# Attention's value products of two units issued as one row, into two halves of one PSUM bank

## The chip, the cores and the metric

The kernel runs on one core of one Trainium2 chip. The metric is the device time of one execution in microseconds (us); the time of a kernel is the median of its runs. The profile is one execution taken by the hardware profiler. Its engines are TensorE (PE; its weight loads are listed apart, as PEld), VectorE (DVE), ScalarE (ACT), GpSimd (POOL) and the queues that issue DMAs, above all SyncE's (SP).

## The reference

Two layers of a block that mixes a 1024-token grid (16 rows of 64) and 256 context tokens in three ways: neighbourhood attention with 8 heads, a bidirectional mLSTM and a Hyena long convolution. What the change touches is the attention:

```python
def row_block(r):
    ...
    s = jnp.concatenate([s_lat..., s_ctx], axis=-1)
    p = jax.nn.softmax(s, axis=-1).astype(v.dtype)
    ...
    o = jnp.einsum('bhjqic,bijchd->bjqhd', p_lat, vw) + jnp.einsum('bhjqn,bnhd->bjqhd', p_ctx, vc)
```

Around it stand `mod = silu(c) @ w_ada + b_ada` (shift, scale and gate of a layer), the input projection `h @ w_in`, and `y @ w_out` with a norm and a gate. In layer 0 the context tokens go through an attention of their own as well. All is in float32.

## The kernel before

All PE work stands in one fixed order, made when the program is built. Each part of the block is a Python generator; `flow` keeps a list of them sorted by rank and lets the first one go on whose time has come by `Clock`, a model of the engines that is advanced as instructions are written down. A generator hands back the tiles it needs, a name that another one will `announce`, or a time; `want` waits until a PSUM bank of a tag is free by that model (`BANKS`: two of `pj`, three of `s`, two of `tp`, one of `o`). So a change in one generator moves the rows of all others. DVE, ACT, POOL and the DMA queues run in the order that comes out too.

- `projections` (rank 2, the last) fills every gap with the input projection: `pj` tiles, each 8 steps of 3 fp32r products, 128x512 or 128x256 wide. 2496 such products belong to layer 0, 1968 to layer 1. The last blocks of a layer (24, 22, 25 and 23: gates of the mLSTM output) end in tiles `sz` and `so` that are written to the DRAM tensor `yp`.
- `na` is the attention. `keys` and `values` load a head; four copies of `work` (rank 1) take units in turn: 8 heads x 5 units in layer 0 (four blocks of 16 grid columns and the context), 8 x 4 in layer 1. A unit makes scores (`apl`, `apc`), a softmax on DVE, ACT and POOL (`ae`), 10 transposes (`apt`, in three groups; a context unit has one group of 4) that are copied to `ph`, and the value products `apo`. These use 64 of the 128 columns of the array, so two of them, one for PSUM partitions 0 to 63 and one for 64 to 127, run side by side; a group is such a pair, 256 or (third group) 128 wide. An fp32 product is two instructions in the trace, so a pair is four. ACT copies one half of the result to `at`, DVE adds it to the other half into `ay`. When a pair of heads is done ("closing"), `az` is `ay` times a gate, and goes to `yp`.
- In `before` the three groups of a unit alternate with the transposes of the next group and with waits for the neighbouring unit (`pv...`), and each group is issued when its `ph` part is there.
- `ada_late` (rank 1.2, after `work`) runs in layer 0's attention: 16 groups `ada`, each 8 products of 32 columns on two tiles `wada` of 512 KB. There are two such tiles in all, so the loads of a group wait for the products of the group before. Each group takes a `tp` bank. Its end (`adas`) is awaited before the attention counts as done (`N0`).
- `out_early` loads `w_out` (8 tiles `wos`, four at a time), splits it (`woh` on ACT; `wol` on DVE for every second one if `N` of the layer is known by then, else all on POOL), as soon as `P` (projections written down) or `N` is known. Then `out_proj` runs the products `op` on `yh`, `yl`, made from `gr`, which is loaded from `yp`.

```python
            raw = []
...
            (nc.vector if i % 2 and f"N{l}" in self.known else nc.gpsimd).tensor_tensor(out=wl[:, b, :], in0=raw[i], in1=wh[:, b, :].bitcast(F32), op=ALU.subtract)
```

The two lines that set the pace of `ada_late`:

```python
                    tiles.append(pool.tile([128, 1024], F32, name=f"wada_{l2}_{part2}_{kt2}", tag="wad", bufs=2))
...
                yield tiles[j], tiles[j + 1], 1.0
                yield from self.want("tp")
```

Of the kernel before, what the change touches and what calls it, by code (L numbers as in the profile page):

```python
# [13 lines left out]
F32 = mybir.dt.float32  # L14
# [3 lines left out]
ALU = mybir.AluOpType  # L18
# [5 lines left out]
L, LC = 1024, 256  # L24
LT = L + LC
# [8 lines left out]
QA, KA, VA, ZA = 0, 4, 8, 12  # L34
# [126 lines left out]
class Kern:  # L161
# [1085 lines left out]
    def na(self, l, pool, upd):  # L1247

        nc = self.nc
        HP = [slice(0, 64), slice(64, 128)]  # L1250
        heads, vals, ys, bias, left = {}, {}, {}, {}, {}
# [61 lines left out]
        def work():  # L1313
            while units:
                turn = 8 * nu - len(units)
                hd, cb = units.pop(0)
                pr, h = hd // 2, hd % 2
                p, o = HP[h], HP[1 - h]
                nme = f"{l}_{hd}_{cb}"
                types = [hf * 3 + (0 if cb == 0 else (2 if cb == 3 else 1)) for hf in range(2)] if cb < 4 else []  # L1320
                for ty in types:
                    if (hd, ty) not in bias:
                        bias[hd, ty] = pool.tile([128, 384], F32, name=f"ab{l}_{hd}_{ty}", tag="ab", bufs=3)
                        nc.sync.dma_start(out=bias[hd, ty], in_=self.I["nab"][l, hd, ty])
# [2 lines left out]
                    ys[hd] = ys[hd + 1] = pool.tile([128, LT], F32, name=f"ay{l}_{pr}", tag="ay", bufs=1)  # L1327
                y = ys[hd]
                qs, kh, kl = heads[hd]
                yield from self.want("s", qs, kh, kl, extra=2.0)  # L1330
                pc = self.bank("s", f"apc{nme}")
                E = []
                st = pool.tile([128, 8, 2], F32, name=f"ast{nme}", tag="ast", bufs=3)
                lat = cb < 4
                q0 = cb * 256 if lat else L
                pls = []
                for hf in range(2):
                    q = qs[:, q0 + hf * 128:q0 + hf * 128 + 128]
                    if lat:
                        cs = slice(CB_START[cb], CB_START[cb] + 32)  # L1340
# [31 lines left out]
                a, b, f = slice(0, 256), slice(256, 512), slice(0, 256)  # L1372
                groups = [([blk(0, 3), blk(1, 3), blk(0, 4), blk(1, 4)], [(0, a, f), (1, b, f)])]
# [3 lines left out]
                ng = len(groups)  # L1377
                closing = h == 1 and cb == nu - 1
                ne = LT if upd else L
                parts = []  # L1380

                for gi in range(ng + 1):
                    if turn and gi < ng:
                        yield f"pv{l}_{turn - 1}_{min(gi + 1, 2)}"
                    if gi < ng:
                        yield from self.want("tp")
                        tp = self.bank("tp", f"apt{nme}_{gi}")
                        for j, x in enumerate(groups[gi][0]):
                            self.tr(out=tp[:, j * 128:(j + 1) * 128], in_=x, identity=self.ident)
                        x = pool.tile([128, 512], F32, name=f"ph{nme}_{gi}", tag="ph", bufs=3)  # L1390
                        w = len(groups[gi][0]) * 128
                        (nc.vector.tensor_copy if gi == 1 else nc.scalar.copy)(x[:, :w], tp[:, :w])
                        parts.append(x)
                    if gi == ng - 1 and closing:
                        yield f"b{l}_{ZA + pr}"
                        zs = []
                        for x in range(0, ne, ne // 2):
                            z = pool.tile([128, 640], F32, name=f"az{l}_{pr}_{x}", tag="ae", bufs=8)[:, 0:ne // 2]
                            nc.sync.dma_start(out=z, in_=self.GT[l][pr][:, x:x + ne // 2])
                            zs.append((slice(x, x + ne // 2), z))  # L1400
                    if gi == 0:
                        continue
                    if gi == 1:
                        if turn:
                            yield f"pv{l}_{turn - 1}_3"
                        yield f"hv{l}_{hd}_{cb if lat else -1}"
                        vc, vb = vals[hd, -1], vals.get((hd, cb))
                        yield from self.want("o", vc)
# [7 lines left out]
                for gi in range(ng, 4):  # L1416
                    self.announce(f"pv{l}_{turn}_{gi}")
                self.announce(f"nv{l}_{hd}_{cb}")
                t = pool.tile([128, 256], F32, name=f"at{nme}", tag="at", bufs=2)
                nc.scalar.copy(t[p], po[o, 0:256])  # L1420
                if lat:
                    yv = grid(y)[p, :, 16 * cb:16 * cb + 16]
                    shp = lambda t: t.rearrange("p (r c) -> p r c", c=16)
                else:
                    yv, shp = y[p, L:LT], lambda t: t
                nc.vector.tensor_tensor(out=yv, in0=shp(po[p, 0:256]), in1=shp(t[p]), op=ALU.add)
# [13 lines left out]
        for w in range(4):  # L1440
            self.spawn(work(), 1)
# [541 lines left out]

# [9 lines left out]
```

## Time and profile before

| what | value |
|---|---|
| median of 3 runs | 1974.19 us (1967.37 to 1975.5) |
| the profiled execution | 1969.88 us, of it 1968.1 us from first to last instruction |
| PE busy | 1857.6 us, 94% of the span |
| DVE, ACT, POOL busy | 1058.3, 786.8, 461.3 us (54%, 40%, 23%) |
| mean granted PE clock | 0.976 |

The profiled execution is 4.3 us below the median. The attention of layer 0 runs from about 680 to 992 us, that of layer 1 from about 1560 to 1840 us. A busy PE is not yet a PE at its peak: what a product really holds up is read from the distance between the starts of two instructions.

### The profile page before, as it was taken

To read this page: it belongs to the slowest core of one execution; us is meant where nothing else is said; L and a number is where in the kernel's file an instruction comes from. 1 tells how busy PE (TensorE), PEld (TensorE's weight loads), DVE (VectorE), ACT (ScalarE), POOL (GpSimd) and SP (SyncE) were. 2 spreads that over 40 slices of the span, in tenths; PEclk is the share of its full clock that TensorE was granted. 3 is DMA by queue.
4 is the path that set the end of the run, shared out by engine and by line. 5 is a ranking of instruction groups with operands and counts; after the bars stand their busy time and mean duration, and the time that the engine had idled before them with its cause. 6 is when DMAs were issued, how large, how long until landed. Compare 5 with 4: busy or idle time off the path is not lost. (4 is left out here: it accounts for less than half of the span.)

```text
span 1968.1 us, 28340 instructions
## 1 busy us (share of the span) xinstructions
PE 1857.6 (94%) x10008; PEld 1418.7 (72%) x10008; DVE 1058.3 (54%) x2398; ACT 786.8 (40%) x1545; POOL 461.3 (23%) x368
## 2 busy tenths in 40 slices
PE   8699989998999899999999999899899999999998
PEld 2465867787788776777777886678677867676776
DVE  3744454537736366677545544444762476666533
ACT  3645342414423254444434444332323255454321
POOL 1534111314220121121222122222412122122300
PEclk9799999999999999999999999999899999999999
DMA  8476888863221557666354357765222455454543
GB/s 315 141 241 211 287 228 242 231 231 107 80 82 45 178 149 216 201 212 217 105 192 139 139 159 217 221 194 172 77 80 82 133 160 161 125 161 131 181 130 107
DMA packets 233610, 328.91 MB, mean 167 GB/s; under 512 B 22509, under 2 KB 162185, under 8 KB 231550
## 3 DMA queue, kind: packets, MB, share of 16 engines
q1 hardware_dynamic: 186942, 264.45, 44.0%
q10 hardware_dynamic: 46528, 62.67, 9.1%
q8 instruction: 79, 1.29, 0.3%
q14 instruction: 61, 0.50, 0.1%
HBM read 230.82 MB, written 96.21 MB: 166 GB/s over the span
## 5 line engine op out<-in xcount | busy, mean ns | idle before, releaser
L182 PE MATMUL pj<-hhi,wh 128*128 128x512 f32 (+2 forms) x1504 | 598.5, 398 | 4.9 <-ACT sv L155 4.9
L182 PE MATMUL pj<-hlo,wh 128*128 128x512 f32 (+2 forms) x1504 | 550.3, 366 | 0.1
L182 PE MATMUL pj<-hhi,wl 128*128 128x512 f32 (+1 forms) x1456 | 535.1, 368 | 0.0
L182 PEld LDWEIGHTS pj<-hhi,wh 128*128 128x128 f32 (+1 forms) x1504 | 285.7, 190 | 71.3 <-issue 29.5
L182 PEld LDWEIGHTS pj<-hlo,wh 128*128 128x128 f32 (+1 forms) x1504 | 285.4, 190 | 46.2 <-issue 9.4
L182 PEld LDWEIGHTS pj<-hhi,wl 128*128 128x128 f32 x1456 | 277.5, 191 | 46.6
L155 POOL TENSOR_TENSOR wl<-wr,wh 128x1024 fp32r<-128x1024 f32 x68 | 165.2, 2429 | 541.1 <-ACT wh L155 511.8
L155 POOL TENSOR_SCALAR ae<-ae,ast 128x640 f32<-128x640 f32 (+1 forms) x72 | 69.4, 964 | 411.0 <-DVE ast L155 313.5
L155 ACT ACTIVATE ae<-ae,ast 128x640 f32<-128x640 f32 (+1 forms) x144 | 113.1, 787 | 106.6 <-DVE ast L155 100.7
L182 PE MATMUL op<-woh,yh 128*128 128x512 f32 x288 | 115.4, 401 | 9.7 <-ACT yh L155 9.7
L182 PE MATMUL apo<-ph,aVn 128*64 128x256 f32 (+1 forms) x800 | 113.7, 369 | 4.0 <-DVE ph L155 1.5
L182 PE MATMUL op<-woh,yl 128*128 128x512 f32 x288 | 114.7, 398 | 0.9 <-DVE yl L155 0.8
L182 PE MATMUL op<-wol,yh 128*128 128x512 f32 x288 | 114.4, 397 | 0.0
L155 ACT CAST wh<-wr 128x1024 fp32r<-128x1024 f32 (+1 forms) x70 | 72.0, 1028 | 103.9 <-PE pj L182 88.6
L155 ACT COPY ph<-apt 128x512 f32<-128x512 f32 (+1 forms) x136 | 65.6, 483 | 112.3 <-PE apt L186 111.8
L186 PE MATMUL apt<-ident,ae 128*128 128x128 f32 x672 | 109.0, 281 | 0.4 <-DVE ph L155 0.3
L186 PEld LDWEIGHTS apt<-ident,ae 128*128 128x128 f32 x672 | 76.9, 141 | 35.8 <-issue 25.1
L155 ACT COPY sr<-pj 128x512 f32<-128x512 f32 (+3 forms) x94 | 49.3, 525 | 133.2 <-PE pj L182 125.3
L155 DVE CUSTOM_DVE_ANT_0 ae<-apl,ab 128x384 f32<-128x384 f32 x128 | 69.5, 552 | 53.8 <-PE apl L182 32.5
L182 PEld LDWEIGHTS apo<-ph,aVn 128*64 128x64 f32 x800 | 40.8, 135 | 53.9 <-issue 29.2
L182 PEld LDWEIGHTS op<-woh,yh 128*128 128x128 f32 x288 | 55.5, 193 | 21.8 <-ACT yh L155 10.6
L182 PEld LDWEIGHTS op<-woh,yl 128*128 128x128 f32 x288 | 55.4, 192 | 14.2 <-DVE yl L155 2.7
(255 smaller groups left out, 3030.4 us busy)
## 6 DMA issues: line engine op xcount, KB each, us to landing
wr<-in_wblk SPq DMA_DIRECT2D x68, 512.0 KB
wada<-in_wada SPq DMA_DIRECT2D x48, 512.0 KB
ab<-in_nab SPq DMA_DIRECT2D x96, 192.0 KB
pr<-sr ACTq DMA_DIRECT2D x64, 256.0 KB
k<-ks SPq DMA_DIRECT2D x128, 128.0 KB
raw<-pr SPq DMA_DIRECT2D x20, 512.0 KB
ark<-pr SPq DMA_DIRECT2D x32, 320.0 KB
gr<-yp SPq DMA_DIRECT2D x18, 512.0 KB
```

The source lines that it names most:

```text
L155: r = emit(*args, **kw)
L182: self.nc.tensor.matmul(o, lhsT=lhsT, rhs=rhs, start=start, stop=stop)
L186: self.nc.tensor.transpose(out=out, in_=in_, identity=identity)
```

## The change

The value products of a unit are kept back until two units have their probabilities transposed; then all groups of both are issued in one row, the first unit into columns 0 to 255 of the one `o` bank, the second into 256 to 511. The three `ph` tiles of a unit become one of 1280 columns (four of them in place of three of 512), and space is made by a smaller scratch for DMA descriptors. ACT copies `at` once for two units of one head (64 partitions x 512), DVE adds twice as before. Scores (`sc...`), transposes (`at...`) and products (`pv...`) of the units are now each written down in the units' order.

```diff
@@ work, before the scores @@
+                if turn > 1:
+                    yield f"sc{l}_{turn - 2}"
...
+                if turn:
+                    yield f"sc{l}_{turn - 1}"
                 yield from self.want("s", qs, kh, kl, extra=2.0)
...
+                self.announce(f"sc{l}_{turn}")
...
@@ work, from the transposes on @@
+                if turn:
+                    yield f"at{l}_{turn - 1}"
+                if turn >= 4:
+                    yield f"pv{l}_{(turn - 4) | 1}"
+                ph = pool.tile([128, 1280], F32, name=f"ph{nme}", tag="ph", bufs=4)
                 parts = []
-                for gi in range(ng + 1):
-                    if turn and gi < ng:
-                        yield f"pv{l}_{turn - 1}_{min(gi + 1, 2)}"
-                    if gi < ng:
-                        yield from self.want("tp")
-                        tp = self.bank("tp", f"apt{nme}_{gi}")
-                        for j, x in enumerate(groups[gi][0]):
-                            self.tr(out=tp[:, j * 128:(j + 1) * 128], in_=x, identity=self.ident)
-                        x = pool.tile([128, 512], F32, name=f"ph{nme}_{gi}", tag="ph", bufs=3)
...
-                    if gi == 1:
-                        if turn:
-                            yield f"pv{l}_{turn - 1}_3"
...
-                        po = self.bank("o", f"apo{nme}")
-                    v = vc if gi == 1 else vb
-                    x = parts[gi - 1]
-                    yield x, v, 0.5
-                    for i, (t, s, os) in enumerate(groups[gi - 1][1]):
-                        self.mm(po[HP[i], os], lhsT=v[:, t, :], rhs=x[:, s], start=gi == 1, stop=gi == ng, beside=i > 0)
-                    self.announce(f"pv{l}_{turn}_{gi - 1}")
...
+                for gi in range(ng):
+                    yield from self.want("tp")
+                    tp = self.bank("tp", f"apt{nme}_{gi}")
+                    for j, x in enumerate(groups[gi][0]):
+                        self.tr(out=tp[:, j * 128:(j + 1) * 128], in_=x, identity=self.ident)
+                    w = len(groups[gi][0]) * 128
+                    x = ph[:, gi * 512:gi * 512 + w]
+                    (nc.vector.tensor_copy if gi == 1 else nc.scalar.copy)(x, tp[:, :w])
+                    parts.append((x, groups[gi][1]))
+                self.announce(f"at{l}_{turn}")
+                pend.append(SimpleNamespace(parts=parts, hd=hd, cb=cb, lat=lat, y=y))
+                if turn % 2 == 0:
+                    continue
+                two = pend[:]
+                pend.clear()
...
+                if turn > 1:
+                    yield f"pv{l}_{turn - 2}"
...
+                yield from self.want("o", *[v for u in two for v in u.vs if v is not None], *[x for u in two for x, _ in u.parts], extra=0.3)
+                po = self.bank("o", f"apo{nme}")
+                for j, u in enumerate(two):
+                    for gi, (x, prods) in enumerate(u.parts):
+                        for i, (t, s, os) in enumerate(prods):
+                            self.mm(po[HP[i], j * 256 + os.start:j * 256 + os.stop], lhsT=u.vs[gi][:, t, :], rhs=x[:, s], start=gi == 0, stop=gi == len(u.parts) - 1, beside=i > 0)
+                self.announce(f"pv{l}_{turn}")
+                t = pool.tile([128, 512], F32, name=f"at{nme}", tag="at", bufs=2)
...
@@ kernel @@
-    nc = bacc.Bacc("TRN2", target_bir_lowering=False, num_devices=1)
+    nc = bacc.Bacc("TRN2", target_bir_lowering=False, num_devices=1, dynamic_dma_scratch_size=1024)
```

What this does to the order, in three places. First PE at the last unit of layer 1's last head (`apo1_7_3`); before, the end of its work, `pj` being the projection that fills in:

```order
L186 MATMUL avt1_7_3_16849<-ident_109,av1_7_3_16793 128x128 x2
L182 MATMUL apo1_7_3_16853<-ph1_7_3_0_16834,aVn1_7_4_16556 64x256 x2
L186 MATMUL apt1_7_3_2_16856<-ident_109,ae1_7_3_0_16676 128x128
L186 MATMUL apt1_7_3_2_16856<-ident_109,ae1_7_3_1_16683 128x128
L182 MATMUL pj1_22_0_16818<-hhi1_9664,wh1_22_16534 128x512
L182 MATMUL pj1_22_0_16818<-hlo1_9665,wh1_22_16534 128x512
L182 MATMUL pj1_22_0_16818<-hhi1_9664,wl1_22_16535 128x512
L182 MATMUL pj1_22_0_16818<-hhi1_9664,wh1_22_16534 128x512
L182 MATMUL pj1_22_0_16818<-hlo1_9665,wh1_22_16534 128x512
L182 MATMUL pj1_22_0_16818<-hhi1_9664,wl1_22_16535 128x512
L182 MATMUL apo1_7_3_16853<-ph1_7_3_1_16841,aVn1_7_3_16796 64x256 x2
L182 MATMUL apo1_7_3_16853<-ph1_7_3_2_16859,aVn1_7_3_16796 64x128 x2
```

Now, the row of units 7_2 and 7_3:

```order
L182 MATMUL pj1_25_0_16679<-hlo1_9460,wh1_25_16570 128x512
L182 MATMUL pj1_25_0_16679<-hhi1_9459,wl1_25_16571 128x512
L182 MATMUL apo1_7_3_16683<-ph1_7_2_16499,aVn1_7_4_16444 64x256 x2
L182 MATMUL apo1_7_3_16683<-ph1_7_2_16499,aVn1_7_2_16599 64x256 x2
L182 MATMUL apo1_7_3_16683<-ph1_7_2_16499,aVn1_7_2_16599 64x128 x2
L182 MATMUL apo1_7_3_16683<-ph1_7_3_16522,aVn1_7_4_16444 64x256 x2
L182 MATMUL apo1_7_3_16683<-ph1_7_3_16522,aVn1_7_3_16637 64x256 x2
L182 MATMUL apo1_7_3_16683<-ph1_7_3_16522,aVn1_7_3_16637 64x128 x2
L182 MATMUL pj1_25_0_16679<-hhi1_9459,wh1_25_16570 128x512
L182 MATMUL pj1_25_0_16679<-hlo1_9460,wh1_25_16570 128x512
```

Two pairs and the pair before them, which stood apart, are now in one row with the three pairs of the neighbour. Counted over the whole program, `apo` products stand in 186 rows before (172 of one pair and 14 of two; 98 in layer 0, 88 in layer 1) and in 36 now (20 and 16; 28 of six pairs and 8 of four). The last row of layer 0 stood after 2376 of its 2496 projections and stands after 2289 now; that of layer 1 had 129 projections left behind it and has 93 now.

Second, PE at the end of layer 0, where the last projections (`pj0_23`) meet the output products (`op0`). Before:

```order
L182 MATMUL pj0_23_1024_9568<-hhi0_373,wl0_23_9293 128x256
L182 MATMUL pj0_23_1024_9568<-hhi0_373,wh0_23_9292 128x256
L182 MATMUL pj0_23_1024_9568<-hlo0_374,wh0_23_9292 128x256
L182 MATMUL pj0_23_1024_9568<-hhi0_373,wl0_23_9293 128x256
L182 MATMUL op0_0_0_9598<-woh0_9396,yh0_0_9541 128x512
L182 MATMUL op0_0_0_9598<-wol0_9397,yh0_0_9541 128x512
L182 MATMUL op0_0_0_9598<-woh0_9396,yl0_0_9542 128x512
```

Now:

```order
L182 MATMUL pj0_23_1024_9271<-hlo0_374,wh0_23_9056 128x256
L182 MATMUL pj0_23_1024_9271<-hhi0_373,wl0_23_9057 128x256
L182 MATMUL ada1_1_2_9314<-wada_1_1_2_9242,cs_106 32x256 x4
L182 MATMUL ada1_1_2_9314<-wada_1_1_3_9244,cs_106 32x256 x4
L182 MATMUL ada1_1_4_9344<-wada_1_1_4_9324,cs_106 32x256 x4
L182 MATMUL ada1_1_4_9344<-wada_1_1_5_9326,cs_106 32x256 x4
L182 MATMUL ada1_1_6_9366<-wada_1_1_6_9354,cs_106 32x256 x4
L182 MATMUL ada1_1_6_9366<-wada_1_1_7_9356,cs_106 32x256 x4
L186 MATMUL adat_1_8_9376<-ident_109,mada1_1_9188 128x128 x2
L182 MATMUL ada1_2_0_9392<-wada_1_2_0_9383,cs_106 32x256 x4
L182 MATMUL ada1_2_0_9392<-wada_1_2_1_9385,cs_106 32x256 x4
L182 MATMUL ada1_2_2_9406<-wada_1_2_2_9402,cs_106 32x256 x4
```

Behind these rows come five more of `ada1_2` and then the same `op0`. Before, all 16 `ada` groups stood among the units, the last with 168 projections still to come; now 4 stand among the units, 5 among the last projections, and 7 between the last projection and the first `op0`. From `op0` on, PE's order is the same up to the attention of layer 1 (but for one transpose pair).

Third, SP's queue at the same place, the loads of `w_out`. Before:

```order
L155 DMA wos0_0_9398<-in_wout 128x1024
L155 DMA wos0_1_9400<-in_wout 128x1024
L155 DMA wos0_2_9402<-in_wout 128x1024
L155 DMA wos0_3_9404<-in_wout 128x1024
L155 DMA wos0_4_9430<-in_wout 128x1024
L155 DMA yp0_83<-so0_25_0_9438 128x512
L155 DMA wos0_5_9454<-in_wout 128x1024
L155 DMA wos0_6_9464<-in_wout 128x1024
L155 DMA wos0_7_9481<-in_wout 128x1024
L155 DMA yp0_83<-so0_25_512_9512 128x512
L155 DMA gr0_0_9539<-yp0_83 128x8x128
L155 DMA gate0_0_9551<-gsc0_6880 128x1024
```

Now:

```order
L155 DMA yp0_83<-so0_25_1024_9296 128x256
L155 DMA wos0_1_9308<-in_wout 128x1024
L155 DMA wos0_2_9310<-in_wout 128x1024
L155 DMA wos0_3_9312<-in_wout 128x1024
L155 DMA wada_1_1_4_9324<-in_wada 128x1024
L155 DMA wada_1_1_5_9326<-in_wada 128x1024
L155 DMA wos0_4_9330<-in_wout 128x1024
L155 DMA wos0_5_9334<-in_wout 128x1024
L155 DMA wos0_6_9338<-in_wout 128x1024
L155 DMA wos0_7_9342<-in_wout 128x1024
L155 DMA wada_1_1_6_9354<-in_wada 128x1024
L155 DMA wada_1_1_7_9356<-in_wada 128x1024
```

The loads of `ada` now stand between those of `w_out`. Behind these rows follow the loads of the other four groups, and among them four small loads `gp`, four `mada`, then `gr0_1` and `wr1_26` (which waits for `yl` on DVE). All eight `wol` of layer 0 are on POOL now; before, four were on DVE.

## Rows read from the trace of the kernel before

**Rows 1.** The page, part 1: busy time, share of span, instructions

```profile
PE 1857.6 (94%) x10008; PEld 1418.7 (72%) x10008; DVE 1058.3 (54%) x2398; ACT 786.8 (40%) x1545; POOL 461.3 (23%) x368
```

**Rows 2.** Both attentions by window: busy PE, PEld, DVE, ACT, POOL; clock; DMA

```profile
687.00:985.00 298.00, 294.43 (x1989) 213.51 (x1988) 198.17 (x601) 145.66 (x315) 57.79 (x49) 1.00 0.61 184
1580.00:1840.00 260.00, 253.68 (x1521) 184.16 (x1522) 166.38 (x508) 127.81 (x267) 54.69 (x41) 0.99 0.47 141
```

**Rows 3.** Timeline of PE, rows of one pair: start, length, instruction

```profile
769.99 0.65 PE L182 MATMUL apo<-ph,aVn 128*64 128x256 f32 x4
770.58 0.38 PE L182 MATMUL pj<-hhi,wh 128*128 128x256 f32 x1
770.80 0.28 PE L182 MATMUL pj<-hlo,wh 128*128 128x256 f32 x1
770.92 0.28 PE L182 MATMUL pj<-hhi,wl 128*128 128x256 f32 x1
...
781.35 0.39 PE L182 MATMUL pj<-hlo,wh 128*128 128x512 f32 x1
781.58 0.39 PE L182 MATMUL pj<-hhi,wl 128*128 128x512 f32 x1
781.90 0.65 PE L182 MATMUL apo<-ph,aVn 128*64 128x256 f32 x4
...
785.24 0.60 PE L186 MATMUL apt<-ident,ae 128*128 128x128 f32 x4
785.77 0.44 PE L182 MATMUL apo<-ph,aVn 128*64 128x128 f32 x4
786.14 0.66 PE L186 MATMUL apt<-ident,ae 128*128 128x128 f32 x4
```

**Rows 4.** Timeline of PE, a row of two pairs and what follows it

```profile
1668.24 0.87 PE L182 MATMUL apo<-ph,aVn 128*64 128x256 f32 x8
1669.04 0.45 PE L182 MATMUL apl<-kh,qs 128*128 128x384 f32 x1
```

**Rows 5.** The same window as Rows 2, tile ada alone: PE, PEld, DVE

```profile
687.00:985.00 298.00, 17.13 (x256) 6.68 (x256) 6.71 (x16) 1.00 0.61 184
```

**Rows 6.** Timeline of SP's queue, first loads of w_out in layer 0

```profile
996.83 7.71 SPq L155 DMA_DIRECT2D wos<-in_wout  x5
```

**Rows 7.** Timeline of ACT, their first use: idle before and its releaser in brackets

```profile
1000.65 2.08 ACT L155 CAST woh<-wos 128x1024 fp32r<-128x1024 f32 x2 [2.50 <-DMA wos<-in_wout]
```

**Rows 8.** Tile wos, its readers: duration ns min/median/max

```profile
L155 ACT CAST woh<-wos x16: 1039/1053/1057, 1000.7 to 1862.8; 128x1024 fp32r<-128x1024 f32 x16
L155 POOL TENSOR_TENSOR wol<-wos,woh x8: 2396/2474/3382, 1001.8 to 1862.7; 128x1024 fp32r<-128x1024 f32 x8
```

**Rows 9.** Timeline of PE at the first output products of either layer

```profile
1013.86 0.28 PE L182 MATMUL pj<-hhi,wl 128*128 128x256 f32 x1
1018.75 0.80 PE L182 MATMUL op<-woh,yh 128*128 128x512 f32 x1 [4.61 <-ACT yh L155]
...
1871.29 0.54 PE L182 MATMUL op<-woh,yh 128*128 128x512 f32 x1 [2.85 <-ACT yh L155]
```

**Rows 10.** Windows around the first output products of layer 0, columns as Rows 2

```profile
1018.70:1025.20 6.50, 6.42 (x14) 4.61 (x15) 1.23 (x1) 0.95 (x1) 0.00 (x0) 0.51 0.64 221
1025.20:1031.70 6.50, 6.50 (x30) 5.37 (x29) 1.23 (x1) 1.84 (x4) 0.53 (x1) 1.00 0.22 81
```

**Rows 11.** Chain that ended last, from layer 1's last value product: start, us

```profile
1838.18 0.82 PE apo L182 x8
...
1841.21 2.09 DMA yp<-az
...
1844.86 5.10 DMA wos<-in_wout
...
1853.75 5.01 DMA gg<-ys
...
1863.80 6.32 DMA gr<-yp
...
1870.19 1.05 ACT yh L155
```

More of the change, by code (lines that the diff above doesn't have):

```diff
@@ L1250, in na @@
         HP = [slice(0, 64), slice(64, 128)]
-        heads, vals, ys, bias, left = {}, {}, {}, {}, {}
+        heads, vals, ys, bias, left, pend = {}, {}, {}, {}, {}, []
         units = [(hd, cb) for hd in range(8) for cb in (0, 1, 2, 3, 4)[:5 if upd else 4]]
@@ L1379, in work @@
                 ne = LT if upd else L
-                parts = []
-                for gi in range(ng + 1):
-                    if turn and gi < ng:
-                        yield f"pv{l}_{turn - 1}_{min(gi + 1, 2)}"
-                    if gi < ng:
-                        yield from self.want("tp")
-                        tp = self.bank("tp", f"apt{nme}_{gi}")
-                        for j, x in enumerate(groups[gi][0]):
-                            self.tr(out=tp[:, j * 128:(j + 1) * 128], in_=x, identity=self.ident)
-                        x = pool.tile([128, 512], F32, name=f"ph{nme}_{gi}", tag="ph", bufs=3)
[L1391 to L1402, printed above, removed]
-                    if gi == 1:
-                        if turn:
-                            yield f"pv{l}_{turn - 1}_3"
-                        yield f"hv{l}_{hd}_{cb if lat else -1}"
-                        vc, vb = vals[hd, -1], vals.get((hd, cb))
-                        yield from self.want("o", vc)
-                        po = self.bank("o", f"apo{nme}")
-                    v = vc if gi == 1 else vb
-                    x = parts[gi - 1]
-                    yield x, v, 0.5
-                    for i, (t, s, os) in enumerate(groups[gi - 1][1]):
-                        self.mm(po[HP[i], os], lhsT=v[:, t, :], rhs=x[:, s], start=gi == 1, stop=gi == ng, beside=i > 0)
-                    self.announce(f"pv{l}_{turn}_{gi - 1}")
@@ L1416, in work @@
[L1416 to L1425, printed above, removed]
@@ L1426, in work @@
-                nc.vector.tensor_tensor(out=yv, in0=shp(po[p, 0:256]), in1=shp(t[p]), op=ALU.add)
+                if turn:
[3 more added lines that the diff above has]
+                ph = pool.tile([128, 1280], F32, name=f"ph{nme}", tag="ph", bufs=4)
+                parts = []
+                for gi in range(ng):
[7 more added lines that the diff above has]
+                    parts.append((x, groups[gi][1]))
@@ new lines, in work @@
+                self.announce(f"at{l}_{turn}")
[4 more added lines that the diff above has]
+                pend.clear()
+                if closing:
+                    yield f"b{l}_{ZA + pr}"
+                    zs = []
+                    for x in range(0, ne, ne // 2):
+                        z = pool.tile([128, 640], F32, name=f"az{l}_{pr}_{x}", tag="ae", bufs=8)[:, 0:ne // 2]
+                        nc.sync.dma_start(out=z, in_=self.GT[l][pr][:, x:x + ne // 2])
+                        zs.append((slice(x, x + ne // 2), z))
@@ new lines, in work @@
+                if turn > 1:
+                    yield f"pv{l}_{turn - 2}"
+                for u in two:
+                    yield f"hv{l}_{u.hd}_{u.cb if u.lat else -1}"
+                    u.vs = [vals[u.hd, -1]] + [vals.get((u.hd, u.cb))] * 2
+                yield from self.want("o", *[v for u in two for v in u.vs if v is not None], *[x for u in two for x, _ in u.parts], extra=0.3)
[4 more added lines that the diff above has]
+                            self.mm(po[HP[i], j * 256 + os.start:j * 256 + os.stop], lhsT=u.vs[gi][:, t, :], rhs=x[:, s], start=gi == 0, stop=gi == len(u.parts) - 1, beside=i > 0)
@@ new lines, in work @@
+                self.announce(f"pv{l}_{turn}")
+                t = pool.tile([128, 512], F32, name=f"at{nme}", tag="at", bufs=2)
+                for j, u in enumerate(two):
+                    self.announce(f"nv{l}_{u.hd}_{u.cb}")
+                    p, o = HP[u.hd % 2], HP[1 - u.hd % 2]
+                    cs = slice(j * 256, j * 256 + 256)
+                    if two[0].hd != two[1].hd:
+                        nc.scalar.copy(t[p, cs], po[o, cs])
+                    elif j == 0:
+                        nc.scalar.copy(t[p], po[o])
+                    if u.lat:
+                        yv = grid(u.y)[p, :, 16 * u.cb:16 * u.cb + 16]
+                        shp = lambda t: t.rearrange("p (r c) -> p r c", c=16)
+                    else:
+                        yv, shp = u.y[p, L:LT], lambda t: t
+                    nc.vector.tensor_tensor(out=yv, in0=shp(po[p, cs]), in1=shp(t[p, cs]), op=ALU.add)
```

## The prediction

> **What bounds the kernel now.** The page's busy times come first: PE is busy for 94% of the span, DVE for 54%, all others for less [rows 1]. A share of busy time is a mean, so next the two attentions alone: PE 294.4 of 298 us and 253.7 of 260, DVE 198 and 166, the DMA engines about half [rows 2]. There PE lacks nothing, because projections stand in every gap of its fixed order. What PE is spared in an attention therefore comes off the end of that layer's projections, as long as nothing else is late by then. So I ask first what the change takes from PE, then what meets PE at the end of either layer. Lengths of PE instructions overlap, so I read distances between starts.
>
> **What a row costs.** Projections start 0.23 us apart; from the last of them to a row of `apo` it is 0.32, so entering costs 0.09 [rows 3]. A row of one pair lasts 0.59 (256 wide: 769.99 to 770.58) or 0.37 (128 wide: 785.77 to 786.14) [rows 3]. A row of both kinds together lasts 0.80 [rows 4]: 0.15 less than 0.58 and 0.37 apart. Leaving costs 0.10 towards a projection (0.22 to the next start against 0.12 after it) and 0.06 towards four transposes (0.66 against 0.60) [rows 3]. Of the 186 rows before, half are followed by transposes, so leaving costs 0.08 in the mean. A row fewer spares 0.15 + 0.09 + 0.08 = 0.32 us. The order has 36 rows for 186, with the same 200 pairs in them: 150 x 0.32 = **48 us less**, 25 in layer 0 and 23 in layer 1. Bounds: 45 (all leave towards transposes) to 52 (all towards projections, 0.16 inside). Rows of six pairs are not in the trace; I take it that pairs three to six follow as the second does.
>
> **The end of layer 0.** The order shows what pays for this. Seven of the 16 `ada` groups now stand between the last projection and `op0`, with nothing else for PE to do. Among the units they cost PE 17.13 / 16 = 1.07 us each [rows 5], all loads hidden. Now each waits for its own load, since there are two tiles and the loads of a group wait for the products of the one before. A 512 KB load takes 3.8 us from issue (996.83) to the cast that waited for it (1000.65) [rows 6, 7], 5.1 with others in flight [rows 11]. From the last projection:
> - Group one: its loads go out during the last 45 narrow projections (45 x 0.12 = 5.4 us), one behind a write that waits for DVE. It is done at about 2 us.
> - Group two: its loads stand on SP behind four `wos`, which cannot start before the last projection, as their tiles lie where its input was. Issue at 3 to 4, 5.1 to land, the products: 10 us.
> - Group three: its loads stand behind `wos` 4 to 7, each of which waits for a `wol`, all on POOL now: 3.8 for the first load, 1.05 for its cast, 4 x 2.45 on POOL [rows 8] = 14.7. Then 5.1 to land and the products: 21 us.
> - Groups four to seven: a tile's turn is 3.8 to load, 0.3 to release and issue, and four products. After an idle time of 4.6 us [rows 9] the granted clock was 0.51 for 6.5 us, the lower level, and 14 products stood where 30 did in the next 6.5 us [rows 10]. A PE that idles through most of the tail will run its groups at that level: 2.1 us for a group, half of it in a tile's turn. 4 x 5.2 = 21, and 1 more because the very last load stands behind `wr1_26`, which waits for `yl`. In all **43 us**.
>
> Before, it was 4.9 us from the last projection to `op0` [rows 9]. The groups' 7 x 1.07 = 7.5 us no longer lie among the units. Net: 43 - 4.9 - 7.5 = **30.6 us more**. Bounds for the 43: 32 (no wait for POOL, full clock, 4.4 a turn) to 52 (seven turns as long as the slowest such load, `gr` with 6.3 [rows 11], and its products).
>
> The Trainium skill ("DMA: Bandwidth & Descriptors", Anatomy of one DMA) gives 2.0 us plus the bytes at 436 GB/s, an estimate of 3.2 us for such a load. By it the last four turns would be 0.6 shorter each, and the sum 2.4 us lower; the row has 3.8, and I stay with it.
>
> Five more groups stand among the last projections, 21 to 54 of them apart. 21 x 0.23 is 4.8 us, less than a turn of 5.2, and SP has writes and a 5.0 us load (`gg` [rows 11]) in between: I take two waits of 2 us, **4 more** (0 to 8).
>
> **The end of layer 1.** Before, a chain runs from the last value product through `az`, `yp`, the `w_out` loads, `gg` stuck behind them on SP, and `gr`, to the first `op`: it starts at 1838.2 [rows 11], and PE waits 2.85 us at its end [rows 9]. Now 93 projections follow the last row, not 129: 21 us of cover, not 30. But `gg` goes out ahead of the `w_out` loads, so the chain shrinks to: `at`, `ay`, `az` 2.9; `yp` 2.1; eight loads, the last of which goes out some 13 us after the first (3.8 to land, 1.05 for the cast, two `wol` of 2.45 [rows 8], and 3 for other work ahead of them on DVE and ACT); 1.4 for four issues; `gr` 6.3; `yh` 1.05. That is 27 us, so PE waits 6 in place of 2.85: **3 more** (0 to 8).
>
> **Slack.** Attention now has less PE time to hide the others in: in layer 0, DVE's 198 us of work fall into some 250 us, 79% against 66%. Before, waits inside both attentions came to 3.6 + 6.3 us [rows 2]. I add **4** (nothing, if waits for single `ph` parts vanish, to 15). ACT has 32 copies fewer and is no bound. The smaller DMA scratch belongs to no queue that this kernel uses for its loads: 0. From `op0` to the second attention the order is the same: 0.
>
> **Sum.** -48 + 30.6 + 4 + 3 + 4 = -6.4 us on the profiled execution, 1969.9, so 1963.5. That run lies 4.3 us under the median of 1974.2; by the median the forecast is **1968 us**. About 0.5% (10 us) is what a measurement can tell from no change here, so this is within it, on the fast side.
>
> **Rivals.**
> - *The tail is short* (chance 0.22): loads that come back in 3.8 us or less, POOL not in the way, no waits added elsewhere: -48 + 19.6 + 3 = -25, so 1949 us. For it: in the tail DMA has little else to move. Against it: `wos` 4 to 7 stand ahead of group three on SP, whatever the loads take.
> - *SP decides the tail* (0.16), the one that ends slower: each of the last four groups' loads also stands behind small loads, `gr0_1` or `wr1_26`, and each such wait is paid in full, as nothing else feeds PE. At 49 us from last projection to `op0` the change gains nothing; at 60, with 4 us more per turn, it is +11, so 1985 us. For it: SP works in order, and `wr1_26` waits for a load, a cast and a subtraction. Against: only that one waits long.
> - *Slack is the price* (0.10): DVE at near 80% in layer 0 makes PE wait for scores and probabilities, 16 us in place of 4: +6, so 1980 us. Against: before, DVE was idle for a third of that time [rows 2], and PE waited for 3.6 us in all.
> - *Rows cost nothing* (0.02): if weights for the other tile shape were loaded during the products before, a row would stream on and merging would spare nothing: +42, so 2016 us. The Trainium skill ("TensorE: Matmul & The Clock Gate", The mechanism) describes such a pull-ahead of weight loads. The rows speak against it [rows 3, 4]: one pair starts 0.09 late, and a second pair in the same row comes 0.15 cheaper.
>
> **Chances and range.** The forecast has 0.50; around it 1956 to 1980. Below 1964.3 (faster by over 0.5%) lie most of the short tail and two fifths of the forecast: 0.41. Above 1984 lie most of the SP case, the last rival and the forecast's edge: 0.17. In between: 0.42. The range for 8 in 10 takes in the bounds of the tail on both sides: 1947 to 1988 us.
>
> **What would show it.** In the changed profile: `apo` in 36 rows, 2.3 us long for six pairs (2 x (0.43 + 0.43 + 0.21) + 0.16), with no wait inside. The last projection of layer 0 at 1014 - 25 - 7.5 + 8 or less (two waits, half of the slack), so near 987 us; then a PE that is idle for some 30 to 35 us between `ada` groups, with waits for `wada` that the profile before hardly has, at the lower clock; `op0` near 1030. The last row of layer 1 to `op` about 27 us. I am wrong if a long row stalls, if the groups of the tail come every 3 us or every 8, or if PE idles more than 10 us inside an attention.

## The result, and the profile after

The changed kernel takes 1995.33 us (median of 6 runs, 1985.5 to 1999.64), the kernel before 1974.85 beside it: ratio 1.010, 95% interval 1.007 to 1.013. That is slower by 1.0%, where 1968 us, 0.3% faster, was forecast, and above the upper end of the range (1988). The profiled run of after took 1999.64, the longest of its six; before's took 1969.88. Nine of these 29.8 us lie ahead of the first attention, where both programs have the same order on PE: the first score product starts at 686.5 us instead of 677.7. In other profiled runs with that same order it came between 676.5 and 683.6, so this is spread between executions.

The page of after: busy time, share of the span and instructions, to set beside [rows 1].

```profile
PE 1826.0 (91%) x10008; PEld 1434.9 (72%) x10008; DVE 1051.6 (53%) x2394; ACT 780.9 (39%) x1513; POOL 467.0 (23%) x372
```

PE does less, in a longer span. Next, windows that cut either layer at the last value row and at the last projection (columns: window, length, then PE, PEld, DVE, ACT and POOL busy, granted clock, DMA share, GB/s). First before, then after.

```profile
677.00:991.50 314.50, 310.19 (x2060) 225.62 (x2060) 206.11 (x627) 151.66 (x327) 61.13 (x50) 0.99 0.60 182
991.50:1013.90 22.40, 22.40 (x124) 19.29 (x120) 13.56 (x12) 10.31 (x14) 8.40 (x4) 1.00 0.65 238
1570.00:1838.70 268.70, 260.91 (x1572) 191.05 (x1572) 173.88 (x531) 132.25 (x274) 56.90 (x42) 0.99 0.48 143
1838.70:1868.00 29.30, 29.30 (x134) 24.16 (x131) 17.70 (x14) 12.19 (x15) 13.36 (x5) 1.00 0.72 247
```

```profile
686.00:963.60 277.60, 258.86 (x1777) 213.62 (x1777) 195.24 (x603) 145.01 (x306) 58.60 (x49) 0.98 0.53 157
963.60:1015.20 51.60, 49.16 (x292) 37.43 (x289) 13.71 (x23) 5.88 (x10) 2.42 (x2) 0.93 0.50 171
1608.70:1866.50 257.80, 248.75 (x1607) 204.79 (x1607) 176.90 (x530) 131.56 (x261) 57.91 (x43) 0.99 0.50 150
1866.50:1887.70 21.20, 21.20 (x98) 17.46 (x95) 13.16 (x12) 7.20 (x9) 7.89 (x4) 1.00 0.61 210
```

Layer 1 shows the gain by itself: PE's work falls from 260.9 + 29.3 to 248.8 + 21.2, by 20.3 us, and the stage from 298.0 to 279.0. In layer 0 PE's work falls by 24.6 (332.6 to 308.0), but its waiting time rises from 4.3 to 21.2 us, and the granted clock falls to 0.98 and 0.93, so that the stage gives back only 7.7.

A value row of after on PE (the idle time before an instruction and its releaser stand in brackets where there is any):

```profile
783.29 0.40 PE L182 MATMUL pj<-hhi,wl 128*128 128x512 f32 x1
783.62 2.38 PE L182 MATMUL apo<-ph,aVn 128*64 128x256 f32 x24
785.93 0.45 PE L182 MATMUL apl<-kh,qs 128*128 128x384 f32 x1
```

2.31 us from start to start for six pairs, entered in 0.33, with no wait inside, as the row's price had it. Now the end of layer 0, from the last projection to `op0`:

```profile
1015.20 0.28 PE L182 MATMUL pj<-hhi,wl 128*128 128x256 f32 x1
1015.41 1.07 PE L182 MATMUL ada<-wada,cs 128*32 128x256 f32 x16
1026.44 2.24 PE L182 MATMUL ada<-wada,cs 128*32 128x256 f32 x16 [9.96 <-DMA wada<-in_wada]
1038.31 2.22 PE L182 MATMUL ada<-wada,cs 128*32 128x256 f32 x16 [9.63 <-DMA wada<-in_wada]
...
1043.08 1.08 PE L182 MATMUL ada<-wada,cs 128*32 128x256 f32 x8 [1.32 <-DMA wada<-in_wada]
1045.44 1.08 PE L182 MATMUL ada<-wada,cs 128*32 128x256 f32 x8 [1.28 <-DMA wada<-in_wada]
...
1060.75 1.08 PE L182 MATMUL ada<-wada,cs 128*32 128x256 f32 x8 [1.62 <-DMA wada<-in_wada]
1061.76 0.80 PE L182 MATMUL op<-woh,yh 128*128 128x512 f32 x1
```

46.6 us where 4.9 stood [rows 9]. In this stretch, and in the first 6.5 us of `op0`, windows show the clock (the last column but two):

```profile
1015.40:1061.70 46.30, 14.61 (x115) 3.30 (x114) 7.99 (x13) 11.78 (x12) 19.99 (x9) 0.56 0.75 258
1061.70:1068.20 6.50, 6.50 (x25) 5.20 (x22) 1.26 (x2) 1.05 (x1) 1.91 (x2) 0.74 0.27 87
```

What PE waited for in layer 0 between 690 and 1014 us (total, times, longest); before, the waits there came to 3.6 us [rows 2]:

```profile
PE apt L186 <- ACT ph L155: 7.3, 7, 2.9
PE apc L182 <- DVE ast L155: 6.0, 4, 2.8
PE ada L182 <- DMA wada<-in_wada: 2.4, 1, 2.4
PE apl L182 <- DVE ast L155: 2.1, 1, 2.1
PE apt L186 <- DVE aVn L155: 1.7, 3, 0.9
PE apt L186 <- DVE ast L155: 1.1, 1, 1.1
```

The longest of DVE's, at a closing unit, in the timeline of PE and of DVE:

```profile
766.72 0.38 PE L182 MATMUL apc<-kh,qs 128*128 128x256 f32 x1 [2.82 <-DVE ast L155]
```

```profile
762.99 0.69 DVE L155 COPY ph<-apt 128x512 f32<-128x512 f32 x1 [0.50 <-PE apt L186]
763.71 0.77 DVE L155 TENSOR_TENSOR ay<-apo,at 64x256 f32<-64x256 f32 x2
764.51 1.56 DVE L155 TENSOR_TENSOR az<-az,ay 128x640 f32<-128x640 f32 x2
766.10 0.56 DVE L155 CUSTOM_DVE_ANT_0 ae<-apl,ab 128x384 f32<-128x384 f32 x1
```

PE's next scores need the bank that the last line reads. DVE comes to it only after the row's two `ay` and the closing's two `az`. Last, the chain at the end of layer 1, to set beside [rows 11] (start, length, what):

```profile
1869.86 3.52 DMA yp<-az
...
1874.82 6.01 DMA wos<-in_wout
...
1886.34 6.81 DMA yp<-so
...
1893.17 6.81 DMA gr<-yp
...
1900.05 1.05 ACT yh L155
...
1901.15 1.22 PE op L182 x2
```

`gg` is gone from the chain, as forecast, and another DMA stands in its place: a write of `yp` from `so`, which SP issues at 1886.34, behind the last `w_out` load, and for whose landing the load of `gr` waits. PE waits 13.0 us before `op` instead of 2.85 [rows 9]:

```profile
1901.15 0.80 PE L182 MATMUL op<-woh,yh 128*128 128x512 f32 x1 [13.02 <-ACT yh L155]
```

### The profile page after: what moved, and what is told of

It is laid out like the page before. It is cut to its first block, busy times and chain, and to the rows that moved or that the text cites. A ratio compares the mean times of both kernels' runs of the same rounds, so it can differ in the third digit from the quotient of the medians.

```text
span 1997.8 us, 28211 instructions
## 1 busy us (share of the span) xinstructions
PE 1826.0 (91%) x10008; PEld 1434.9 (72%) x10008; DVE 1051.6 (53%) x2394; ACT 780.9 (39%) x1513; POOL 467.0 (23%) x372
## 4 chain that ended last, share of the span: by engine, by line
PE 36%; DMA 8%; DVE 6%; issue 3%; ACT 2%; POOL 1%; SPq 0%; ACTq 0%; DVEq 0%; POOLq 0%
PE pj L182 15%; PE op L182 10%; PE apo L182 2%; PE h L182 2%; PE apt L186 2%; DVE ae L155 2%; DMA wada<-in_wada 2%; DMA raw<-pr 1%; PE apl L182 1%; ACT ae L155 1%; PE ada L182 1%; DMA wos<-in_wout 1%; PE apc L182 1%; PE mpn L182 1%; DMA pr<-sr 1%
## 5 line engine op out<-in xcount | busy, mean ns | idle before, releaser
L186 PE MATMUL apt<-ident,ae 128*128 128x128 f32 x672 | 101.7, 275 | 14.6 <-ACT ph L155 8.7
L182 PE MATMUL apo<-ph,aVn 128*64 128x256 f32 (+1 forms) x800 | 80.6, 350 | 0.0
L182 PEld LDWEIGHTS apo<-ph,aVn 128*64 128x64 f32 x800 | 52.1, 137 | 27.9 <-issue 8.5
L182 PE MATMUL ada<-wada,cs 128*32 128x256 f32 (+1 forms) x320 | 38.0, 543 | 36.9 <-DMA wada<-in_wada 36.7
```

What stands on the lines that cost most here:

```text
L182: self.nc.tensor.matmul(o, lhsT=lhsT, rhs=rhs, start=start, stop=stop)
L186: self.nc.tensor.transpose(out=out, in_=in_, identity=identity)
```

## The experiments

**The ada groups first.**

```diff
-                self.spawn(self.ada_late(pool), 1.2)
+                self.spawn(self.ada_late(pool), 0.95)
```

> The changed kernel with the ada groups put ahead of the attention's units again: all 16 stand among the units, none behind the last projection, and 78 projections follow the last value row of layer 0. Theory 1 (the tail is the largest loss): the 46.6 us from the last projection to op0 fall to some 5, the seven groups cost 7.5 among the units, so 34 less: near 1961 us, faster than before the change. Theory 2 (the chain behind the last value row takes over, as at the end of layer 1): from that row to op0 it was 33 us before, and 78 projections cover only 18, so PE waits about 14 before op0 and the gain is 25: near 1970. Theory 3 (waits inside the attention are the largest loss, the tail only moved idle time): the idle time inside layer 0's attention grows by most of what the tail gave: above 1985.

Measured: 1958.96 us, ratio to before 0.991 (0.989 to 0.994). Windows of layer 0 and the first `op`:

```profile
683.00:989.80 306.80, 296.48 (x2100) 239.80 (x2102) 199.63 (x628) 147.59 (x312) 61.69 (x50) 0.99 0.62 188
989.80:1002.70 12.90, 12.90 (x81) 11.37 (x78) 5.25 (x9) 3.60 (x6) 0.95 (x1) 1.00 0.65 231
```

```profile
1012.98 0.80 PE L182 MATMUL op<-woh,yh 128*128 128x512 f32 x1 [10.00 <-ACT yh L155]
```

The time is that of theory 1, by a way that none of the three had whole. The chain does take over before `op0`, as theory 2 says, but PE waits 10.0, not 14. Against that, PE's waits inside the attention shrink, from 20.6 us in the list above to 9.1, against theory 3. With the same work on PE as before apart from the rows, PE is busy for 309.4 us in place of 332.6: the rows of layer 0 gave 23.2. Not all of the tail is gained, though: from the first to the last `op` of layer 0 it is 128.8 us here and 119.1 in the changed kernel, with 8.5 and 1.4 us of waiting inside.

**The tail alone, in the kernel before.**

```diff
+                if j >= 18:
+                    yield "P0"
                 yield tiles[j], tiles[j + 1], 1.0
```

> The kernel before with one line more: ada groups 10 to 16 wait until all projections of layer 0 are in the order, so that seven groups follow the last projection; the value products stay as they were. Theory 1 (the tail costs what the profile of the changed kernel shows, whatever the value products do): from the last projection to op0 45 to 50 us instead of 4.9, 7.5 less among the units, so 34 more: near 2009 us, ratio 1.017. Rival (the tail in the changed kernel is long only because its attention also ran late or left other loads in the queue): under 30 us from last projection to op0, 1990 or less.

Measured: 2000.02 us, ratio 1.014 (1.010 to 1.018), 24 us more than before. From the last projection (1007.85) to `op0` (1051.93) it is 44.1 us, near theory 1, without any change to the value products. The whole costs less than 34: PE's work up to the last projection falls from 332.6 to 322.8, so seven groups cost 9.8 among the units, not 7.5 (each is also a row of another tile shape, which may make the difference; no run shows it apart), and the `op0` stage is 4.7 shorter.

**The small DMA scratch alone, in the kernel before.**

```diff
-    nc = bacc.Bacc("TRN2", target_bir_lowering=False, num_devices=1)
+    nc = bacc.Bacc("TRN2", target_bir_lowering=False, num_devices=1, dynamic_dma_scratch_size=1024)
```

> The kernel before, with the smaller DMA scratch alone. The changed kernel's profile reached its first attention 8.8 us later than before's, with the same order of instructions up to there. Theory 1 (spread between executions): no change, 1974 within 4 us, first attention at 678 within 4. Rival (the smaller scratch, or the addresses that it moves, slows the first stages): 6 to 9 us more, near 1982.

Measured: 1974.56 us, ratio 0.9995 (0.998 to 1.001); the first score product starts at 680.2. Theory 1: the scratch costs nothing that this interval shows, and the later start of after was spread.

**The last gated writes of layer 1 from ACT, in the changed kernel.**

```diff
-            nc.sync.dma_start(out=d[:, c0:c0 + w], in_=t[:, :w])
+            (nc.scalar if l else nc.sync).dma_start(out=d[:, c0:c0 + w], in_=t[:, :w])
```

> The changed kernel, with the last gated writes of layer 1 (yp from so) issued by ACT instead of SP, where one stood behind eight w_out loads until 1886.3 and the load of gr waited for it to land. Theory 1 (that write is what made the end of layer 1 longer): gr goes out right behind the w_out loads, 6 to 7 us earlier, PE waits some 7 in place of 13.0 before op of layer 1: near 1989 us, ratio to the changed kernel 0.997. Rival (the w_out loads and their casts set the end anyway): PE still waits 12 to 13, no change.

Measured: 1988.14 us (10 runs), ratio to before 1.007 (1.005 to 1.010). SP's queue at the end of layer 1:

```profile
1860.93 13.18 SPq L155 DMA_DIRECT2D wos<-in_wout  x8
1874.16 0.43 SPq L155 DMA_DIRECT2D gr<-yp  x1
```

`gr` now goes out right behind the `w_out` loads, and PE waits 6.85 before `op` in place of 13.0: theory 1. The time itself is 7 us below the changed kernel's, as it should be, but the intervals of the two overlap; it is the wait that decides.

**One copy of each unit from DVE to ACT, the order kept.**

```diff
-                    (nc.vector.tensor_copy if gi == 1 else nc.scalar.copy)(x, tp[:, :w])
+                    if gi == 1:
+                        nc.scalar.engine.copy(x, tp[:, :w])
+                        self.clock.issue("vector", "tensor_copy", (x, tp[:, :w]), {})
+                    else:
+                        nc.scalar.copy(x, tp[:, :w])
```

> The changed kernel with PE's order kept row for row, and the copy of each unit's second group of transposes moved from DVE to ACT: DVE has some 0.6 us less per unit (20 of its 195 us in layer 0's attention), ACT 0.6 more. Theory 1 (DVE's load is what PE waits for inside the attention): the waits for DVE (scores, 8 us) shrink to under 3, the idle time of layer 0's attention falls from 21.8 by 5 or more: 1988 or less. Theory 2 (the waits come from three transposes of a unit in two PSUM banks, each behind whatever its copying engine does first): the waits of the transposes for ACT (7.3) grow by more than DVE's shrink: 1995 or more.

Measured: 1990.48 us, ratio 1.007 (1.004 to 1.010), between the two theories; the interval overlaps that of the changed kernel, so the waits have to decide. The waits, between 690 and 1007 us:

```profile
PE apc L182 <- DVE ast L155: 5.5, 3, 2.6
PE apt L186 <- ACT ph L155: 5.1, 5, 1.7
```

DVE did 20.5 us less in the stretch 686 to 1013 (187.6 for 208.1), and PE's waits for DVE's scores stayed. That drops theory 1. Those for ACT's copies, three forms of them together (5.1 + 2.9 + 0.8), came to 8.8 for 7.3, which is no clear rise either, with 16 us more work on ACT. From the first score to the last projection of layer 0, PE's waiting came to 20.5 us in all, for 20.7 in the changed kernel. So the amount of work on either engine is not what sets most of it.

**The closing products from DVE to POOL, the order kept.**

```diff
-                        nc.vector.tensor_tensor(out=z, in0=z, in1=y[:, x], op=ALU.mult)
+                        nc.gpsimd.engine.tensor_tensor(out=z, in0=z, in1=y[:, x], op=ALU.mult)
+                        self.clock.issue("vector", "tensor_tensor", (), dict(out=z, in0=z, in1=y[:, x]))
```

> The changed kernel with PE's order kept row for row, and the gate products of each closing head pair (az, two of 0.8 us) moved from DVE to POOL. Moving 20 us of copies off DVE left the waits for scores as they were (5.9 for 6.0), so the amount of DVE's work is not what PE waits for. Theory 1 (place in the queue: right behind a two-unit row DVE does ay and az, 2.3 us, ahead of the scores that PE needs next): the two longest waits for scores in layer 0 (2.82 and 2.55, each at a closing) fall by 1.6 each, the sum of such waits from 6.0 to under 3.5; some 3 us less inside layer 0's attention, time 1990 to 1996. Theory 2 (some other load or the transposes set these two waits): they stay at 2.5 or more.

Measured: 1985.5 us, ratio 1.006 (1.003 to 1.008), a little below what was expected. The profiled run is 14.7 us shorter than that of the changed kernel, and 10.0 of this is an early start of its first attention, at 676.5; the 4.7 behind that are the size expected. The waits, between 683 and 1008 us:

```profile
PE apt L186 <- ACT ph L155: 6.9, 7, 2.5
PE apl L182 <- DVE ast L155: 2.6, 1, 2.6
PE apc L182 <- DVE ast L155: 2.4, 3, 1.2
```

The two waits at the closings (`apc`) are now 1.23 and 0.95, each 1.6 less, and the sum fell from 6.0 to 2.4: theory 1. The first of them:

```profile
756.26 0.39 PE L182 MATMUL apc<-kh,qs 128*128 128x256 f32 x1 [1.23 <-DVE ast L155]
```

The other wait for scores, near the start of the attention (`apl`), is no closing and stayed (2.6 for 2.1). A few us of DVE's work, taken from ahead of the scores, did what 20 us taken from elsewhere did not. The Trainium skill ("Perfetto Trace Analysis", Tensor Engine Instruction) calls DVE and ACT strictly first in, first out; for DVE these two runs agree, as 1.56 us of `az` taken from ahead of the awaited scores made each wait 1.6 shorter. For ACT no run here shows it. The edit did something beyond its aim as well: at the end of layer 1 PE waits 10.0 us before `op` in place of 13.0.

**The price of a row.** Two kernels on the base of the ada groups first; eight more products between the two units of each row. The control has `False` in place of `b % 2 == 0`.

```diff
                 for j, u in enumerate(two):
+                    for b in range(8 if j else 0):
+                        a, c = (po[:, 256:272], self.zz) if b % 2 == 0 else (po[HP[0], 256:272], self.zz[:, 0:64])
+                        nc.tensor.matmul(a, lhsT=c, rhs=self.ident[:, 0:16], start=True, stop=True)
                     for gi, (x, prods) in enumerate(u.parts):
```

> The control for the next run. The kernel with the ada groups first, and in each of the 36 value rows eight extra products of 16 columns between the two units, all with half of PE's columns as the value products have (weights zero, into a part of the bank that the second unit overwrites). No change of tile shape is added, so it costs only the products: between 36 x 8 x 0.03 = 9 and 36 x 8 x 0.12 = 35 us (0.12 is a product of 128 columns), so 1968 to 1994 us.

> As the control, with the same 16 columns and the same places, but every second of the eight products uses all of PE's columns: 4 x 36 = 144 more changes from half to full tile and back. Theory 1 (a row's price is the change of tile shape, 0.32 us for out and back): 144 x 0.32 = 46 us more than the control. Rival (the gain of merged rows came from fewer separate starts, waits or weight loads, not from the shape): within 5 us of the control.

Measured: 1992.48 and 2041.06 us. The control costs 33.5 more than its base, 0.116 a product; the 144 changes of tile shape and back cost 48.6 on top, 0.34 each, with the full products that they bring. In the timeline of PE, one such row of the control and one of the other (the length is that of the whole group):

```profile
797.59 1.00 PE L1426 MATMUL apo<-ident,zz 128*64 128x16 f32 x15
```

```profile
811.34 2.19 PE L1426 MATMUL apo<-ident,zz 128*128 128x16 f32 x15
```

The same number of products takes more than twice as long when every second one has the other shape. That is not the change alone: the two kernels also differ in that four of the eight products are full ones, and narrow full products come further apart by themselves. In the kernel before, 16 instructions of full products of 64 columns, with no change of shape between them:

```profile
1307.87 1.90 PE L182 MATMUL h<-m1i,s 128*128 128x64 f32 x16
1309.57 0.48 PE L182 MATMUL pj<-hhi,wh 128*128 128x512 f32 x1
```

That is 1.70 us from start to start, 0.21 a product of two instructions, where a half one of the control takes 0.116. If a full product of 16 columns costs about the same, then 0.10 of the 0.34 is its own length, and the change out and back is left with about 0.24, an estimate from these rows. The rival's 5 us are out either way. A kernel with eight full products in a row, which would measure the change by itself, was not run. So the change of shape makes the larger part of the price of a row, and the rest of it is not told apart.

**Three edits together.** The ada groups first, the last gated writes from ACT, and `wol` on DVE:

```diff
-            (nc.vector if i % 2 and f"N{l}" in self.known else nc.gpsimd).tensor_tensor(out=wl[:, b, :], in0=raw[i], in1=wh[:, b, :].bitcast(F32), op=ALU.subtract)
+            nc.vector.tensor_tensor(out=wl[:, b, :], in0=raw[i], in1=wh[:, b, :].bitcast(F32), op=ALU.subtract)
```

> Three edits on the changed kernel: the ada groups first, the last gated writes of layer 1 issued by ACT, and all eight subtractions that make wol on DVE (1.25 us each) instead of mostly on POOL (2.45). Theory 1 (at the end of both layers SP stands in w_out loads that wait for wol): SP is through them some 5 us earlier in either layer, PE's waits before op fall from 10.0 and 10.5 us to about 5 and 2: near 1946 us. Rival (DVE is shared with the last units, or the loads' own time sets it): only the write's 6 us are gained, near 1953, waits of 10 and 5.

Measured: 1951.36 us, ratio to before 0.987 (0.984 to 0.989): faster than both kernels. The rival has it nearly: PE waits 8.8 and 5.0 us before `op` (10.0 and 10.5 without the two later edits), so `wol` moved little beyond what the write gave.

**A wider margin of the planner** on top of that (`margin = 0.45` in place of 0.3).

> The kernel with the three edits (1951 us) and the planner's margin for every wait at 0.45 us instead of 0.3, so that it puts other PE work between a wait and what is waited for. The order then has 63 and 81 projections behind the last value rows instead of 78 and 93. Theory 1 (waits inside the attention are a few tenths to 2 us that the planner thought covered): 9.7 of idle time inside layer 0's attention falls to 5 or less, but PE waits 3 more before either op since 15 and 12 projections fewer stand there: within 4 us of 1951. Rival (the waits are places in the queues, which a margin does not move): idle time as before and 6 us more, 1957.

Measured: 1983.94 us, ratio 1.005 (1.003 to 1.007). A miss: the margin holds for the whole program, and the first attention began at 713.5 us, 31 later; inside layer 0's attention PE waited 18.5 us, not less but more than the 9.1 of its base. It says nothing for either theory.

## Why the prediction was wrong

By its own terms, on the profiled executions (us):

| term | predicted | measured |
|---|---|---|
| rows | -48 | -43.5 (23.2 from the run with the ada groups first, 20.3 in layer 1) |
| seven groups no longer among units | -7.5 | -9.8 (tail alone) |
| last projection to `op0` | +38.1 | +41.7 |
| layer 0: waits of five groups (4), half the slack (2) | +6 | +16.9 of waits and 8.4 of slower work |
| layer 1: half the slack | +2 | +1.3 |
| end of layer 1 | +3 | +10.2 |
| `op0` stage, and from there to layer 1 | 0 | -5.1 + 0.6 |
| ahead of the first attention | 0 | +8.8, spread between executions |

The predicted terms give -6.4; those measured give 29.5, of the 29.8 by which the profiled runs differ. Without the 8.8 of spread they give 20.7, and the medians differ by 20.5. Two rows make nearly all of the error: the waits and slower work of layer 0 (19.3 us more than reckoned) and the end of layer 1 (7.2 more).

**Rows: right.** 36 rows, 2.3 us, no wait inside, and 43.5 / 150 = 0.29 us came back for a row, where 0.32 was taken. The rival that rows cost nothing is out. A change of tile shape out and back costs about 0.24 by the estimate from the two runs with extra products, so it is most of this price, not shown to be all. The Trainium skill ("TensorEngine Tiling (Array Packing)", Key Properties) says that changing the tiling mode drains TensorE; that a change costs time the two runs show (48.6 us for 144), a drain no run shows.

**The tail: right in kind, 3.6 us short in size.** Group three was done 25 us after the last projection (1038.31 and 2.2, less 1015.20), where it was to be 21; the four turns behind it took 21.2 us, where I had 22. SP issued the loads of groups two and three about when it was reckoned to (3.1 and 15.8 us after the last projection, for 3 to 4 and 14.7), but from there to the products that waited for them it took 8.2 and 7.3 us, not 5.1; for group two (products at 1026.44):

```profile
1018.26 0.92 SPq L155 DMA_DIRECT2D wada<-in_wada  x2
```

The estimate of 3.2 us for such a load, which the prediction works out from the Trainium skill ("DMA: Bandwidth & Descriptors", Anatomy of one DMA), is further off still; that section gives its fit for DMAs that GpSimd issues, and SP issues these. The short-tail rival, and the one in which SP makes the tail 60, are both out. Through most of it the granted clock was 0.56, near the lower of its two levels (1.2 of 2.4 GHz), as reckoned. The tail alone in the kernel before is 44.1 long, so it comes from where the groups stand and not from the value products. Two sizes beside it were missed and cancel in part: the groups cost more among the units (9.8), which a change of tile shape at each may explain, and the `op0` stage got 5 us shorter. In its first 6.5 us the granted clock was 0.74, behind groups that came every 2 to 3 us; before, after 4.6 us of idle time, it was 0.51 [rows 10]; that is 1.5 us. Over the whole stage (1018.7 to 1143 before, 1061.7 to 1180.9 after) the clock was 0.96 and then 0.99, and the waits fell from 2.8 to 1.4 us, which together make nearly all of the 5.

**Slack in layer 0: the step that failed.** I took 4 us of slack for both layers and two waits of 2 for ada groups. Layer 1 bears it out, and so does the one wait for `wada` in layer 0, 2.4 us. But in all layer 0 shows 16.9 us more of waiting, so some 14.5 of slack where I had 2. PE idled for 18.7 us inside that attention (277.6 less 258.9), and more than 10 was named as a sign that the forecast is wrong. The rival "slack is the price" has the size, 16 us, but not the cause. DVE was busy for 195 of 277.6 us, 70%, and 20 us less of its work left the waits for scores as they were. For the two longest of these, what counts is what stands ahead in DVE's queue when PE needs a bank back: two units' `ay` and a closing's `az` ahead of the scores. That such waits are worse when PE has little else between units is argued from one pair of orders, which differ in more than that: with the ada groups in front there are 717 projections in the attention instead of 588, the same work takes 306 us instead of 277, and the waits fall to less than half with DVE's work nearly unchanged (199.6 for 195.2). For the waits for ACT's copies (7.3), the largest entry, the place in the queue is only argued: no run took them away, so what sets them stays open.

**The clock was left out.** PE's work in layer 0 should have fallen by 23.2 + 9.8 = 33.0; it fell by 24.6. The granted clock of 0.98 and 0.93, against 0.99 and 1.00, makes 277.6 x 0.01 + 51.6 x 0.07 = 6.4 of the missing 8.4. Behind the wait of 2.82 us at 766.72, and behind that of 2.4 for an ada group at 986.9, windows show PE busy near the lower level (columns as above):

```profile
768.00:771.60 3.60, 3.60 (x13) 3.12 (x12) 2.62 (x15) 2.33 (x5) 1.01 (x1) 0.53 0.43 132
986.40:993.40 7.00, 6.39 (x26) 3.86 (x27) 0.42 (x1) 0.00 (x0) 0.00 (x0) 0.51 0.60 201
```

So some waits inside an attention are paid a second time, in slower products behind them; not all, as the stretch with a wait of 2.88 us (900 to 930) has 1.00. I had reckoned with that only in the tail.

**The end of layer 1 failed too: the chain was drawn with one link missing.** I let the last writes of `yp` pass, because `gg` went out early. But the write from `so` stands on SP behind all eight `w_out` loads, and `gr` waits until it lands. From the last value product (1866.56) to `op` it was 34.6 us, where I had 27: 6.8 for that write, and `yp` took 3.5 instead of 2.1. Issuing it elsewhere gave 6.2 us back at its place.

Why the change loses, then: its rows are worth 43.5 us. Merged rows let the units run ahead of the planner's rank for the ada groups; the groups land behind the last projection, where 41.7 us of load time have no cover. On top come the waits and slower work of layer 0 and the late write of layer 1, 25.3 and 10.2 us where the forecast had 6 and 3. One number in the rank turns 1995 into 1959.

## What to carry to other kernels

When a change frees the bounding engine, look for the streams of lower rank that used to fill its gaps, and ask where they go: their loads are free only while that engine has other work. Cost a wait in an in-order queue by what stands ahead of it at that moment, not by the engine's busy share. For a write that a later load waits for, count every slow instruction that its queue issues first.

## What was unexpected of the hardware

Going from half to full tile and back costs PE 0.34 us (48.6 us for 144) even for products of 16 columns, of which a half one takes 0.116; about 0.24 of it, by the estimate above, is the change itself, the time of two such products. And layer 0's attention, with single waits of up to 2.9 us, ran at a mean granted clock of 0.98, and the stretch behind it at 0.93, partly at the lower level, where before it was 0.99 and 1.00; that cost some 6 us beside the waits themselves.
